# Attention softmax written to an SBUF page, and the splits of landed squares ordered behind it

## Chip, cores and metric

One core of a Trainium2 chip runs the whole program. The metric is the device time of one execution in microseconds (us). The engines are named as in the profile: PE multiplies matrices, DVE, ACT and POOL work on tiles elementwise, SP issues most DMAs. Each engine runs its instructions strictly in the order in which they stand in its own queue, and waits for the others through semaphores. PE writes to PSUM; DVE and ACT reach both PSUM and SBUF, POOL and the DMAs only SBUF in this kernel.

## Reference

A backbone of two layers over 1024 latent tokens of width 1024 and 256 context tokens, in float32. Layer 0 is windowed attention with a sink logit and 16 query heads on 4 key heads; layer 1 is a gated convolution module. The change touches the attention of layer 0 alone. Cut to what matters:

```python
def block_fn(args):                     # 128 queries of one block, all heads
    qblk, blk = args
    kw = ... # keys of blocks blk-1, blk, blk+1 (384 keys), vw likewise
    s_win = einsum(qblk, kw) * scale; s_win = where(mask, s_win, -inf)
    s_ctx = einsum(qblk, kc) * scale                     # 256 context keys
    p_ctx, p_win = sink_softmax(sink, s_ctx, s_win)      # one softmax over sink, context and window
    return einsum(p_ctx, vc) + einsum(p_win, vw)
...
y = (o * silu(z)) @ w_out
```

## The kernel before

Every float32 product is made of three matmuls on parts: a high part (the value rounded to PE's fp32r type, made by ACT with a copy) and a low part (the rest, made by DVE or POOL with a subtraction), as high*high + high*low + low*high.

**Blocks.** The attention stage walks `steps`, 16 heads x 8 query blocks (`h`, `qb`). A block goes through this chain. `scores` (L1096): six matmuls write 128 queries x up to 640 keys to a PSUM tile `pss` (two such tiles exist, used in turn). DVE scales and masks the scores and takes the maximum (a fused tensor_tensor_reduce, which the profile calls CUSTOM_DVE_ANT, result `sc`), ACT takes the exponential with its sum, DVE the reciprocal, ACT multiplies by it. All of this is done in place in `pss`. `square_up` (L1130): DVE transposes 32 x 32 squares from `pss` to an SBUF page `psq_page`, and a DMA writes that to DRAM (`psq`). `land` (L1149): a DMA reads it back with the squares in place, to one of four slots (qb mod 4) of the SBUF tile `ptlo`. `split_p` (L1155): ACT makes the high part `pthi`, and POOL (slots 0, 1) or DVE (slots 2, 3) the low part in place in `ptlo`; for blocks 3 and 4 a strip of 32 columns goes to `edge` pages as well. `pv` (L1188): when four blocks (a half of a head) are split, 18 matmuls multiply values by the probabilities, into `pso`. Four slots are all there is: the next half lands only when `pv` has read this one.

**Order.** In step i the loop of L1318 emits: `square_up(i)`, the landing of block i-2, `scores(i+1)`, the split of block i-3, then `fill(12)`, that is 12 matmuls of the projection of a later head (tile `psg`, with weight chunks `whi`, `wlo`; 24 matmuls make half a chunk, whose result ACT and DVE or POOL take away: `rope_half` for a query chunk, `zs_page` for a gate chunk), and after every fourth block `pv`. Beside this run the low parts of output weights (`lhi_page`, `low_page`) and sums for the second modulation (`pso<-dww_raw`). PE is pinned to the order of the program (`pin("P")`). On DVE, ACT, POOL and SP a list scheduler places the instructions, by its own estimate of when each can run. `after(ins, anchor)` (L661) ties an instruction behind another in that order, without a semaphore.

**Pages.** SBUF pages of 1024 floats come from a pool of 45, and the page that has been free longest is given out first.

At three places, where the key head changes (`regroup`, L1358, behind heads 3, 7 and 11), whole chunks of keys and values stand between the last scores of one group and its `pv`.

Of the kernel before, what the change touches and what calls it, by code (L numbers as in the profile page):

```python
# [9 lines left out]
F32 = mybir.dt.float32  # L10
F32R = mybir.dt.float32r
AF = mybir.ActivationFunctionType
ALU = mybir.AluOpType

P = 128
# [15 lines left out]
TB = T // P  # L31
# [64 lines left out]
def backbone_kernel(  # L96
# [8 lines left out]
    V, A, G, PE, SY = (InOrder(tc, e) for e in (nc.vector, nc.scalar, nc.gpsimd, nc.tensor, nc.sync))  # L105
# [10 lines left out]
    pg = Pages(pgpool, 45, "page", 1024)  # L116
# [8 lines left out]
    def ps_s():  # L125
        return ps.tile([P, 1024], F32, tag="s", name=nm("pss"), bufs=2)
# [18 lines left out]
    def ctile(shape, dt, name):  # L145
        return cpool.tile(shape, dt, tag=name, name=name, bufs=1)

    def small(shape, dt=F32, name="sm", bufs=2):
        return cpool.tile(shape, dt, tag=f"{name}", name=nm(name), bufs=bufs)

    def act(out, in_, func, **kw):
        return A.activation(out=out, in_=in_, func=func, **kw)

    def tt(eng, out, a, b, op):
        return eng.tensor_tensor(out=out, in0=a, in1=b, op=op)
# [4 lines left out]
    def split_lo(eng, lo, full, hi):  # L160
        return tt(eng, lo, full, hi.bitcast(F32), ALU.subtract)
# [5 lines left out]
    nsink = ctile([P, NH], F32, "nsink")  # L167
# [475 lines left out]
    mask = mask_pg[:, 0:768]  # L643
# [12 lines left out]
    anchor = []  # L656
    anchor_p = []
    anchor_a = []
    anchor_z = []

    def after(ins, anchor=anchor):  # L661
        if anchor:
            tc.add_manual_dep(ins.ins, anchor[0].ins.name, mybir.DependencyInfo(
                mybir.DependencyClass.NoSync, mybir.DependencyReason.DATA), reason="behind the softmax")
# [427 lines left out]
        fillq.append((key, job(key)))  # L1092

    ptile = {}

    def scores(h, qb):  # L1096
        g = h // 4
        q = qt[h]
        kk = kvt[g]
        c = kk[2]  # L1100
        k0, k1 = max(qb - 1, 0), min(qb + 1, TB - 1)
        nw = (k1 - k0 + 1) * P
        s = ps_s()
        w0 = 512 - nw
        qsl = slice(qb * P, qb * P + P)
        ksl = slice(k0 * P, k0 * P + nw)
        for n, (a, b) in enumerate(((0, 0), (0, 1), (1, 0))):
            PE.matmul(s[:, w0:512], q[a][:, qsl], kk[b][:, ksl], start=n == 0, stop=n == 2)
            PE.matmul(s[:, 512:768], q[a][:, qsl], c[:, b], start=n == 0, stop=n == 2)
        sc8 = small([P, 3], name="sc", bufs=6)  # L1110
        nmx, l0, ri = (sc8[:, i:i + 1] for i in range(3))
        w = nw + CT

        act(s[:, 768:769], nsink[:, h:h + 1], AF.Copy)
        sc = dict(scale=-SCALE, scalar=nsink[:, h:h + 1], op0=ALU.add, op1=ALU.min, accum_out=nmx)
        if qb == TB - 1:
            sv = s[:, w0:768].rearrange("p (a b) -> p a b", a=2)
            V.tensor_tensor_reduce(out=sv, in0=sv, in1=mask.rearrange("p (a b) -> p a b", a=2)[:, :, 0:256], **sc)
        else:
            V.tensor_tensor_reduce(out=s[:, w0:768], in0=s[:, w0:768], in1=mask[:, 640 - w:640], **sc)  # L1120
        act(s[:, w0:769], s[:, w0:769], AF.Exp, bias=nmx, scale=-1.0, accum_out=l0)
        V.reciprocal(ri, l0)
        act(s[:, w0:768], s[:, w0:768], AF.Copy, scale=ri)
        ptile[(h, qb)] = s
        if qb == TB - 1:
            pg.free(*qt.pop(h))

# [1 line left out]

    def square_up(h, qb):  # L1130

        s = ptile.pop((h, qb))
        sq = pg.alloc(F32, [1024], "psq")
        st = sq[:, 0:640].rearrange("p (b t j) -> p t b j", b=4, t=5)
        turns = {0: ((256, 1, 4),), TB - 1: ((256, 0, 2), (384, 2, 3))}.get(qb, ((128, 0, 5),))
        for c0, t0, nt in turns:
            anchor[:] = [V.transpose(out=st[:, t0:t0 + nt],
                                     in_=s[:, c0:c0 + nt * P].rearrange("p (t b j) -> p t b j", t=nt, b=4))]
        z = squares[(h * TB + qb) % len(squares)]
        x0 = 32 * int(qb == 0)  # L1140
        SY.dma_start(out=z.rearrange("(p b) x -> p b x", b=4)[:, :, x0:160],
                     in_=sq[:, 0:640].rearrange("p (b x) -> p b x", b=4)[:, :, x0:160])
        pg.free(sq)

    def slot(t, qb):
        x0, ql = 32 * int(qb == 0), qb % 4
        return t[:, ql * 640:ql * 640 + 640].rearrange("p (a x) -> p a x", a=4)[:, :, x0:160]
# [7 lines left out]
    def split_p(h, qb):  # L1155

        hi, lo = (slot(t, qb) for t in (pthi, ptlo))
        raw = lo.bitcast(F32)
        if qb in (3, 4):
            if h % 2 == 0 and qb == 3:  # L1160
                edges[:] = [pg.alloc(F32R, [2, 4, P], "edge")]
            i, t = 2 * (qb - 3) + 1 - h % 2, 64 * (4 - qb)
            eh, el = (edges[0][:, n, i].rearrange("p (a j) -> p a j", a=4) for n in range(2))
            act(eh, raw[:, :, t:t + 32], AF.Copy)
            split_lo(V, el, raw[:, :, t:t + 32], eh)
        anchor_a[:] = [act(hi, raw, AF.Copy)]
        if qb % 4 < LO_POOL:
            anchor_p[:] = [split_lo(G, lo, raw, hi)]
        else:
            anchor[:] = [split_lo(V, lo, raw, hi)]  # L1170

    edges = []

# [89 lines left out]
    for kt in range(KT):  # L1263
# [12 lines left out]
        if 0 < kt < 5:  # L1276
            for _ in range(2):
                b = (KT - len(ctodo)) % 3
# [15 lines left out]
        if kt == KT - 1:  # L1294
            scores(0, 0)
# [22 lines left out]
    for i, (h, qb) in enumerate(steps):  # L1318
# [14 lines left out]
        if nxt and nxt[1] == 0:  # L1333
            fill(1000, ("q", h + 1))
        square_up(h, qb)
        h2, q2 = back(i, 2)
        h3, q3 = back(i, 3)
# [3 lines left out]
        if nxt and not regroup:  # L1341
            scores(*nxt)
        if h3 >= 0 and h3 // 4 == h // 4:
            split_p(h3, q3)
# [13 lines left out]
        if regroup:  # L1358
            g = nxt[0] // 4
            old = kvt[g - 1]  # L1360
            land(h, qb - 1)
            run(job(("k", g)))
            land(h, qb)
            for q in range(qb - 2, qb + 1):
                split_p(h, q)
            run(job(("v", g)))
            pv(h, 1)
            pg.free(*old[:3])
            scores(*nxt)
            continue  # L1370
# [7 lines left out]
    h, qb = NH - 1, TB - 1  # L1378
    land(h, qb - 1)
    split_p(h, qb - 2)  # L1380
    land(h, qb)
    fill(12)
# [649 lines left out]
```

## Time and profile before

| | |
|---|---|
| median of 3 runs | 1804.7 us (1802.41 to 1808.81) |
| the profiled execution: its own time | 1810.56 us |
| its span on the core | 1807.9 us |
| DVE, ACT, POOL busy in the span | 67%, 54%, 49% |
| start of the first `pv` of the profile, start of the last | 110.21 us, 927.63 us |

The attention stage takes about 130 to 940 us of the span; the stages behind it are the output projection of the attention and the convolution layer. The profile is read as follows. A group row has the engine, the operation, the tile written and those read, the shape, the count, and after the bar the busy time in us, the mean time of one in ns, and how long the engine had stood idle before them, with what ended that idle time. A row of the timeline has the start and the length in us, and in square brackets the idle time before it. In a row of stretches each engine's busy time is followed by its number of instructions, and then the mean TensorE clock that was granted (PEclk, 1.00 is the full clock).

### The profile page before, as it was taken

Reading aid. Unit: us, or ns where it says so; the run is one execution under the profiler, and the core shown is the slowest. Engines: PE = TensorE matmul, PEld = TensorE weight load, DVE = VectorE, ACT = ScalarE, POOL = GpSimd, SP = SyncE. Lnnn points to the kernel's source line nnn. Section 1 sums busy time; section 2 is a strip of 40 time slices with the busy share of each in tenths; the row PEclk is TensorE's granted clock in tenths of the full one; section 3 lists DMA queues with packets and bytes.
Section 4 is the critical chain, followed back from the end, with each engine's and each line's share of the span. In section 5 each row is a group of like instructions: output and inputs, shape, how many; then the busy total and the mean of one; then the engine's idle time right before and its main releaser. Section 6 shows DMA issues by size and latency. Waiting matters only on the chain.

```text
span 1807.9 us, 23416 instructions
## 1 busy us (share of the span) xinstructions
PE 1666.5 (92%) x7828; PEld 1386.2 (77%) x7828; DVE 1216.5 (67%) x2227; ACT 972.1 (54%) x1699; POOL 890.6 (49%) x658
## 2 busy tenths in 40 slices
PE   9988799888988789888779999999999999999998
PEld 6776677777777678766668887888888888888887
DVE  5866765565466564567531528999999999986742
ACT  6755555555456554565523435565665656466651
POOL 0345654555545455363200116799988898420310
PEclk9999999988999989999889999999999999999999
DMA  9476766776468665767877762202020212277981
GB/s 380 138 226 221 245 193 195 230 229 217 146 200 265 213 194 171 236 211 213 279 228 268 250 239 82 94 13 82 13 82 24 82 47 67 85 238 230 344 293 59
DMA packets 206936, 326.31 MB, mean 180 GB/s; under 512 B 15722, under 2 KB 114338, under 8 KB 206816
## 3 DMA queue, kind: packets, MB, share of 16 engines
q1 hardware_dynamic: 200736, 314.86, 52.5%
q10 hardware_dynamic: 6080, 9.97, 2.1%
q8 instruction: 61, 1.00, 0.2%
q14 instruction: 59, 0.48, 0.1%
HBM read 231.70 MB, written 82.58 MB: 174 GB/s over the span
## 4 chain that ended last, share of the span: by engine, by line
PE 64%; DMA 17%; DVE 9%; ACT 6%; issue 3%; POOL 1%; SPq 0%; ACTq 0%; DVEq 0%; POOLq 0%
PE psg L90 31%; PE pso L90 18%; PE pss L90 16%; DMA ptlo<-psq 7%; DMA psq<-psq_page 4%; ACT pss L90 2%; DVE psq_page L90 2%; DVE pss L90 1%; ACT pthi L90 1%; DMA dww_raw<-in_ada_w_dram 1%; DMA low_page<-in_conv_w_out_dram 1%; DVE ptlo L90 1%; DVE pso L90 1%; DMA rope_half<-rope_half 1%; ACT lhi_page L90 1%
## 5 line engine op out<-in xcount | busy, mean ns | idle before, releaser
L90 POOL TENSOR_TENSOR odd_half<-odd_half,prod_half 128x513 f32<-128x513 f32 (+2 forms) x252 | 313.8, 1253 | 23.2 <-ACT prod_half L90 10.0
L90 POOL TENSOR_TENSOR wlo_page<-wraw_page,whi_page 128x512 fp32r<-128x512 f32 (+1 forms) x104 | 175.5, 1703 | 234.9 <-ACT whi_page L90 175.6
L90 PE MATMUL psg<-hh_page,whi_page 128*128 128x512 f32 x600 | 246.7, 411 | 0.6 <-DVE kvc_page L90 0.6
L90 PE MATMUL psg<-hl_page,whi_page 128*128 128x512 f32 x600 | 243.9, 407 | 0.0
L90 PE MATMUL psg<-hh_page,wlo_page 128*128 128x512 f32 x600 | 242.8, 405 | 0.0
L90 ACT ACTIVATE pss<-pss,sc 128x640 f32<-128x640 f32 (+3 forms) x256 | 187.5, 735 | 102.6 <-DVE sc L90 98.6
L90 ACT ACTIVATE prod_half<-ubuf,dww 128x513 f32<-128x513 f32 (+2 forms) x252 | 165.4, 675 | 115.5 <-POOL odd_half L90 111.6
L90 PE MATMUL psg<-h2h_page,whi_page 128*128 128x512 f32 x464 | 181.9, 392 | 0.0
L90 PE MATMUL psg<-h2h_page,wlo_page 128*128 128x512 f32 x464 | 180.6, 389 | 0.0
L90 PE MATMUL psg<-h2l_page,whi_page 128*128 128x512 f32 x464 | 180.5, 389 | 0.0
L90 DVE SCALAR_TENSOR_TENSOR pss<-ubuf,dww,pss 128x512 f32<-128x512 f32 (+3 forms) x270 | 172.5, 671 | 0.1
L90 DVE SCALAR_TENSOR_TENSOR pss<-ubuf,wsum,pss 128x512 f32<-128x512 f32 (+3 forms) x270 | 171.8, 671 | 0.2
L90 POOL TENSOR_TENSOR ptlo<-ptlo,pthi 128x512 fp32r<-128x512 f32 (+1 forms) x64 | 103.8, 1628 | 109.1 <-ACT pthi L90 62.2
L90 DVE STREAM_TRANSPOSE psq_page<-pss 128x640 f32<-128x640 f32 (+1 forms) x144 | 106.8, 752 | 68.6 <-ACT pss L90 56.0
L90 PE MATMUL pss<-kh_page,qh_page 128*128 128x384 f32 (+1 forms) x128 | 48.6, 380 | 102.8 <-DVE psq_page L90 79.7
L90 PEld LDWEIGHTS psg<-hh_page,wlo_page 128*128 128x128 f32 x600 | 118.5, 198 | 26.5
L90 PEld LDWEIGHTS psg<-hh_page,whi_page 128*128 128x128 f32 x600 | 120.3, 200 | 22.1 <-DVE kvc_page L90 1.0
L90 PEld LDWEIGHTS psg<-hl_page,whi_page 128*128 128x128 f32 x600 | 119.5, 199 | 20.5
L90 ACT ACTIVATE whi_page<-wraw_page 128x1024 fp32r<-128x1024 f32 x88 | 92.7, 1053 | 69.4 <-PE psg L90 26.4
L90 ACT ACTIVATE pthi<-ptlo 128x640 fp32r<-128x640 f32 (+1 forms) x128 | 91.1, 718 | 58.8 <-DMA ptlo<-psq 57.2
L90 POOL TENSOR_TENSOR low_page<-low_page,lhi_page 128x512 f32<-128x512 f32 x64 | 89.8, 1409 | 63.0 <-ACT lhi_page L90 46.4
L90 PEld LDWEIGHTS pss<-kh_page,qh_page 128*128 128x128 f32 x128 | 25.5, 199 | 123.9 <-issue 115.2
(267 smaller groups left out, 4193.7 us busy)
## 6 DMA issues: line engine op xcount, KB each, us to landing
psq<-psq_page SPq DMA_DIRECT2D x112, 320.0 KB, 4.0
ptlo<-psq SPq DMA_DIRECT2D x112, 320.0 KB, 5.1
wraw_page<-in_k_wconv_dram SPq DMA_DIRECT2D x48, 512.0 KB, 3.7
wraw_page<-in_k_win_dram SPq DMA_DIRECT2D x40, 512.0 KB, 4.3
wol_page<-wolA SPq DMA_DIRECT2D x32, 512.0 KB, 8.3
wo_page<-in_attn_w_out_dram SPq DMA_DIRECT2D x32, 512.0 KB, 6.6
wo_page<-in_conv_w_out_dram SPq DMA_DIRECT2D x32, 512.0 KB, 6.6
wol_page<-wolC SPq DMA_DIRECT2D x32, 512.0 KB, 6.8
```

The source lines that it names most:

```text
L90: r = f(*a, **k)
```

## The change

The masked scores are now written by the fused reduce to an SBUF page `p` (allocated in `scores`, freed in `square_up`); the exponential and the scaling by the reciprocal, both still on ACT, run in place in that page, and the transposes read it. PSUM holds the raw scores only until the reduce has read them. The sink's column is put at the end of the page. Two lists name the newest softmax's reciprocal (`tie_v`, DVE) and scaling (`tie_a`, ACT): the splits on ACT and DVE, and the next block's sink column, are tied behind them. The splits on POOL are not tied. What is computed is the same.

```diff
+    tie_v, tie_a = [], []
...
-        act(s[:, 768:769], nsink[:, h:h + 1], AF.Copy)
+        p = pg.alloc(F32, [1024], "p")
+        after(act(p[:, w:w + 1], nsink[:, h:h + 1], AF.Copy), tie_a)
...
-            V.tensor_tensor_reduce(out=s[:, w0:768], in0=s[:, w0:768], in1=mask[:, 640 - w:640], **sc)
-        act(s[:, w0:769], s[:, w0:769], AF.Exp, bias=nmx, scale=-1.0, accum_out=l0)
-        V.reciprocal(ri, l0)
-        act(s[:, w0:768], s[:, w0:768], AF.Copy, scale=ri)
-        ptile[(h, qb)] = s
+            V.tensor_tensor_reduce(out=p[:, 0:w], in0=s[:, w0:768], in1=mask[:, 640 - w:640], **sc)
+        act(p[:, 0:w + 1], p[:, 0:w + 1], AF.Exp, bias=nmx, scale=-1.0, accum_out=l0)
+        tie_v[:] = [V.reciprocal(ri, l0)]
+        tie_a[:] = [act(p[:, 0:w], p[:, 0:w], AF.Copy, scale=ri)]
+        ptile[(h, qb)] = p
...
-                                     in_=s[:, c0:c0 + nt * P].rearrange("p (t b j) -> p t b j", t=nt, b=4))]
+                                     in_=p[:, c0:c0 + nt * P].rearrange("p (t b j) -> p t b j", t=nt, b=4))]
+        pg.free(p)
...
-            act(eh, raw[:, :, t:t + 32], AF.Copy)
-            split_lo(V, el, raw[:, :, t:t + 32], eh)
+            after(act(eh, raw[:, :, t:t + 32], AF.Copy), tie_a)
+            after(split_lo(V, el, raw[:, :, t:t + 32], eh), tie_v)
         anchor_a[:] = [act(hi, raw, AF.Copy)]
+        after(anchor_a[0], tie_a)
...
             anchor[:] = [split_lo(V, lo, raw, hi)]
+            after(anchor[0], tie_v)
```

The order on PE is the same before and after. On ACT, DVE, POOL and SP most rows of the attention stage move. The first place is ACT where head 9 begins, in the order of before: `pss_6641` is its block 0, `pss_6680` its block 1, and the four rows with `pthi` (one of them twice) split blocks 4 to 7 of head 8.

```order
L90 ACTIVATE pss_6641,sc_6648<-pss_6641,sc_6648 128x513
L90 ACTIVATE edge_page_6578<-ptlo 128x128
L90 ACTIVATE pthi<-ptlo 128x640
L90 ACTIVATE lhi_page_1337<-low_page_6620 128x512
L90 ACTIVATE pss_6641<-pss_6641,sc_6648 128x512
L90 ACTIVATE pthi<-ptlo 128x640
L90 ACTIVATE lhi_page_1337<-low_page_6620 128x512
L90 ACTIVATE pss_6680<-nsink 128x1
L90 ACTIVATE qh_page_6435<-rope_half_6627 128x512
L90 ACTIVATE pthi<-ptlo 128x640 x2
L90 ACTIVATE zs_page_6658<-psg_6659 128x512
L90 ACTIVATE pss_6680,sc_6687<-pss_6680,sc_6687 128x641
```

The same place of the changed kernel, where `p_page_6753` is block 0 and `p_page_6793` block 1 of head 9:

```order
L90 ACTIVATE qh_page_6536<-rope_half_6731 128x512
L90 ACTIVATE p_page_6753,sc_6752<-p_page_6753,sc_6752 128x513
L90 ACTIVATE p_page_6753<-p_page_6753,sc_6752 128x512
L90 ACTIVATE edge_page_6682<-ptlo 128x128
L90 ACTIVATE pthi<-ptlo 128x640
L90 ACTIVATE lhi_page_1347<-low_page_6724 128x512
L90 ACTIVATE p_page_6793<-nsink 128x1
L90 ACTIVATE p_page_6793,sc_6792<-p_page_6793,sc_6792 128x641
L90 ACTIVATE p_page_6793<-p_page_6793,sc_6792 128x640
L90 ACTIVATE pthi<-ptlo 128x640
```

Four splits stood ahead of the exponential of block 1; now one stands there, and the four are spread out, one behind the softmax of each block. The second place is ACT at block 3 of head 9, the last block before the `pv` of head 8's second half, before:

```order
L90 ACTIVATE pss_6762,sc_6769<-pss_6762,sc_6769 128x641
L90 ACTIVATE zs_page_6658<-psg_6739 128x512
L90 ACTIVATE pss_6762<-pss_6762,sc_6769 128x640
L90 ACTIVATE whi_page_6917<-wraw_page_6532 128x1024
L90 ACTIVATE ozs_page_6614<-zs_page_6658 128x256
```

and now, with `p_page_6877` as that block and `psg_6846` as the half chunk whose last matmul stands right ahead of that `pv` on PE:

```order
L90 ACTIVATE p_page_6877,sc_6876<-p_page_6877,sc_6876 128x641
L90 ACTIVATE whi_page_7028<-wraw_page_6635 128x1024
L90 ACTIVATE zs_page_6763<-psg_6846 128x512
L90 ACTIVATE p_page_6877<-p_page_6877,sc_6876 128x640
L90 ACTIVATE pthi<-ptlo 128x640
L90 ACTIVATE lhi_page_1347<-low_page_6859 128x512
```

The split of head 8's block 7 stood ahead of the exponential of block 1; now it is behind the scaling of this block, and a weight chunk's high part has come between the exponential and the scaling. The third place is DVE in the same block of the changed kernel (ISA is the fused reduce and the reading of its result):

```order
L90 ISA p_page_6877,sc_6876<-pss_6869,mask_page_597,nsink 128x640
L90 ISA sc_6876 128x1
L90 STREAM_TRANSPOSE psq_page_6866<-p_page_6829 128x5x4x32
L90 TENSOR_TENSOR ptlo<-ptlo,pthi 128x640
L90 SCALAR_TENSOR_TENSOR pso_951<-dww_raw,cs,pso_951 128x256
L90 RECIPROCAL sc_6876<-sc_6876 128x1
L90 SCALAR_TENSOR_TENSOR pso_951<-wsum_raw,cs,pso_951 128x256
L90 COPY mask_page_597<-pso_951 128x256
L90 SCALAR_TENSOR_TENSOR zs_page_6763<-zs_page_6763,psg_6846 128x512
L90 STREAM_TRANSPOSE psq_page_6925<-p_page_6877 128x5x4x32
L90 TENSOR_TENSOR ptlo<-ptlo,pthi 128x640
```

The low part of block 7 (the last row) now stands behind the reciprocal and the transpose of this block; before, both DVE low parts of that half stood ahead of the reciprocal of block 1.

More of the change, by code (lines that the diff above doesn't have):

```diff
@@ L1112, in scores @@
         w = nw + CT
-        act(s[:, 768:769], nsink[:, h:h + 1], AF.Copy)
+        p = pg.alloc(F32, [1024], "p")
+        after(act(p[:, w:w + 1], nsink[:, h:h + 1], AF.Copy), tie_a)
         sc = dict(scale=-SCALE, scalar=nsink[:, h:h + 1], op0=ALU.add, op1=ALU.min, accum_out=nmx)
         if qb == TB - 1:
-            sv = s[:, w0:768].rearrange("p (a b) -> p a b", a=2)
-            V.tensor_tensor_reduce(out=sv, in0=sv, in1=mask.rearrange("p (a b) -> p a b", a=2)[:, :, 0:256], **sc)
-        else:
-            V.tensor_tensor_reduce(out=s[:, w0:768], in0=s[:, w0:768], in1=mask[:, 640 - w:640], **sc)
-        act(s[:, w0:769], s[:, w0:769], AF.Exp, bias=nmx, scale=-1.0, accum_out=l0)
-        V.reciprocal(ri, l0)
-        act(s[:, w0:768], s[:, w0:768], AF.Copy, scale=ri)
-        ptile[(h, qb)] = s
+            V.tensor_tensor_reduce(
+                out=p[:, 0:w].rearrange("p (a b) -> p a b", a=2),
+                in0=s[:, w0:768].rearrange("p (a b) -> p a b", a=2),
+                in1=mask.rearrange("p (a b) -> p a b", a=2)[:, :, 0:256],
+                **sc)
+        else:
+            V.tensor_tensor_reduce(out=p[:, 0:w], in0=s[:, w0:768], in1=mask[:, 640 - w:640], **sc)
[3 more added lines that the diff above has]
+        ptile[(h, qb)] = p
         if qb == TB - 1:
@@ L1130, in square_up @@
     def square_up(h, qb):
-        s = ptile.pop((h, qb))
+        p = ptile.pop((h, qb))
         sq = pg.alloc(F32, [1024], "psq")
         st = sq[:, 0:640].rearrange("p (b t j) -> p t b j", b=4, t=5)
-        turns = {0: ((256, 1, 4),), TB - 1: ((256, 0, 2), (384, 2, 3))}.get(qb, ((128, 0, 5),))
+        turns = {0: ((0, 1, 4),), TB - 1: ((0, 0, 2), (128, 2, 3))}.get(qb, ((0, 0, 5),))
         for c0, t0, nt in turns:
             anchor[:] = [V.transpose(out=st[:, t0:t0 + nt],
-                                     in_=s[:, c0:c0 + nt * P].rearrange("p (t b j) -> p t b j", t=nt, b=4))]
+                                     in_=p[:, c0:c0 + nt * P].rearrange("p (t b j) -> p t b j", t=nt, b=4))]
+        pg.free(p)
         z = squares[(h * TB + qb) % len(squares)]
```

## The prediction

> **What bounds the kernel now.** I read the page first, then the stretch of the attention stage, then who PE waited for in it, and last the timeline at single waits.
>
> ```profile
> span 1807.9 us, 23416 instructions
> ...
> PE 1666.5 (92%) x7828; PEld 1386.2 (77%) x7828; DVE 1216.5 (67%) x2227; ACT 972.1 (54%) x1699; POOL 890.6 (49%) x658
> ```
>
> ```profile
> 130.00:940.00 810.00, 686.43 (x3286) 579.28 (x3286) 473.30 (x932) 426.73 (x860) 392.33 (x289) 0.93 0.68 215
> ```
>
> PE carries the program. All but a little of its idle time lies in the attention stage: 810.00 - 686.43 = 123.6 us of 1807.9 - 1666.5 = 141.4 us. No other engine is full there (DVE 473 of 810), so the loss is one of latency. The waits of PE in that stage, with total, number and longest:
>
> ```profile
> PE pss L90 <- DVE psq_page L90: 74.7, 31, 5.2
> PE pss L90 <- DVE sc L90: 19.3, 6, 5.3
> ...
> PE pso L90 <- DVE ptlo L90: 7.8, 2, 4.2
> ```
>
> 94.0 us are scores that wait for a `pss` tile, to be released by the transposes of the block two before. 7.8 us are `pv` waiting for a low part. Why the transposes are late shows at the start of head 9 on ACT and DVE:
>
> ```profile
> 544.00 0.31 ACT L90 ACTIVATE edge_page<-ptlo 128x128 fp32r<-128x128 f32 x1 [2.11 <-DMA ptlo<-psq]
> 544.21 0.72 ACT L90 ACTIVATE pthi<-ptlo 128x640 fp32r<-128x640 f32 x1
> 544.84 0.61 ACT L90 ACTIVATE lhi_page<-low_page 128x512 fp32r<-128x512 f32 x1
> 545.36 0.64 ACT L90 ACTIVATE pss<-pss,sc 128x513 f32<-128x513 f32 x1
> ```
>
> ```profile
> 555.87 0.41 PE L90 MATMUL pss<-kh_page,qh_page 128*128 128x384 f32 x1 [3.31 <-DVE psq_page L90]
> ```
>
> ACT stood 2.11 us at a split whose square had not landed, and the exponential behind it in the queue waited too. The delay runs through block 1 to its transpose, and PE stands 3.31 us at the scores of block 3.
>
> A wait costs more than its length. Stretches right behind a wait, then the wait that stood ahead of the second of them:
>
> ```profile
> 152.30:157.70 5.40, 5.40 (x16) 4.53 (x17) 1.81 (x5) 3.13 (x6) 1.80 (x2) 0.50 0.64 218
> 172.20:175.60 3.40, 3.40 (x17) 2.99 (x18) 3.27 (x8) 1.45 (x5) 1.03 (x1) 1.00 0.70 237
> 219.50:222.50 3.00, 3.00 (x10) 2.71 (x11) 3.00 (x6) 1.78 (x5) 2.00 (x2) 0.50 0.58 171
> 384.90:389.80 4.90, 4.90 (x14) 4.22 (x15) 2.17 (x6) 1.83 (x4) 0.41 (x1) 0.50 0.82 255
> 557.10:560.50 3.40, 3.40 (x10) 2.66 (x9) 1.28 (x3) 1.58 (x4) 1.57 (x2) 0.50 0.43 152
> ```
>
> ```profile
> 172.16 0.41 PE L90 MATMUL pss<-kh_page,qh_page 128*128 128x384 f32 x1 [2.73 <-DVE psq_page L90]
> 152.27 0.55 PE L90 MATMUL pss<-kh_page,qh_page 128*128 128x256 f32 x1 [3.96 <-DVE psq_page L90]
> ```
>
> Behind waits of 3.31 and 3.96 us the granted clock is 0.50 for 3.0 to 5.4 us, mean of the four rows with 0.50: 4.2 us, in which half of the time is lost, 2.1 us. Behind 2.73 us it stays 1.00. The stage's mean clock of 0.93 says the same in total: (1 - 0.93) / 0.5 x 810 = 113 us at half clock, so about 57 us lost. The block waits are 101.8 of the 123.6 us idle, so 82% of that, 47 us, is theirs. **At stake: 101.8 + 47 = 149 us.**
>
> A second way: three halves of heads, from one `pv` to another.
>
> ```profile
> 132.55 0.40 PE L90 MATMUL pso<-pthi,kvc_page 128*128 128x512 f32 x1
> ...
> 203.97 0.40 PE L90 MATMUL pso<-pthi,kvc_page 128*128 128x512 f32 x1
> 207.14 0.28 PE L90 MATMUL pss<-kh_page,qh_page 128*128 128x256 f32 x1
> ```
>
> ```profile
> 564.35 0.33 PE L90 MATMUL pss<-kh_page,qh_page 128*128 128x384 f32 x1
> ...
> 565.23 0.40 PE L90 MATMUL psg<-hh_page,whi_page 128*128 128x512 f32 x1
> ...
> 567.96 0.33 PE L90 MATMUL pss<-kh_page,qh_page 128*128 128x384 f32 x1
> ```
>
> (203.97 - 132.55) / 3 = 23.8 us a half. Without waits, scores take 565.23 - 564.35 = 0.88 us and the 12 fill matmuls 2.73, so a step is 3.61 and a half 4 x 3.61 + 3.17 for `pv` + some 0.5 of other matmuls = 18.1 us. Lost: 5.7 us a half. Of 32 `pv`, three stand behind a regroup; 29 x 5.7 = 165 us. I take the middle of the two, **157 us, 5.4 us a half**.
>
> **The change, part by part.** *Removed: the wait of scores for transposes.* The `pss` tile is free when the reduce has read it, and that reduce belongs to a block two steps (7.2 us) older. I cost what is left at nothing; the cover is those two steps.
>
> *Added: the wait of `pv` for the split of its fourth block.* The last split is now tied behind the softmax of the block whose scores stand one fill ahead of `pv`. In that order, on ACT and DVE:
>
> ```profile
> L90 DVE CUSTOM_DVE_ANT_0 pss<-pss,mask_page,nsink 128x640 f32<-128x640 f32 x88 | 77.4, 880 | 23.5 <-ACT pss L90 22.6
> L90 ACT ACTIVATE pthi<-ptlo 128x640 fp32r<-128x640 f32 x105 | 75.9, 730 | 31.2 <-DMA ptlo<-psq 29.8 <-issue 1.2
> L90 DVE TENSOR_TENSOR ptlo<-ptlo,pthi 128x640 fp32r<-128x640 f32 x60 | 75.1, 1255 | 16.9 <-ACT pthi L90 16.2
> L90 DVE STREAM_TRANSPOSE psq_page<-pss 128x640 f32<-128x640 f32 x89 | 74.8, 844 | 39.4 <-ACT pss L90 33.0 <-DMA psq<-psq_page 6.0
> L90 ACT ACTIVATE pss<-pss,sc 128x641 f32<-128x641 f32 x88 | 67.1, 762 | 40.5 <-DVE sc L90 39.5
> L90 ACT ACTIVATE pss<-pss,sc 128x640 f32<-128x640 f32 x88 | 66.8, 762 | 40.1 <-DVE sc L90 38.5 <-DMA wraw_page<-in_k_win_dram 0.9 <-DVE pso L90 0.5
> ...
> L90 ACT ACTIVATE whi_page<-wraw_page 128x1024 fp32r<-128x1024 f32 x33 | 34.8, 1055 | 20.0 <-DVE oz_half L90 8.3 <-PE psg L90 7.1 <-DMA wolC<-low_page 2.1
> ...
> L90 ACT ACTIVATION_READ_ACCUMULATOR pss<-pss,sc 128x1 f32 x117 | 22.7, 194 | 0.0
> ...
> L90 DVE RECIPROCAL sc<-sc 128x1 f32<-128x1 f32 x117 | 18.3, 156 | 59.4 <-ACT pss L90 58.4
> ...
> L90 ACT ACTIVATE zs_page<-psg 128x512 f32<-128x512 f32 x29 | 17.1, 589 | 11.5 <-PE psg L90 11.5
> L90 DVE DVE_READ_ACCUMULATOR2_ANT sc<- 128x1 f32 x117 | 16.2, 139 | 0.0
> ```
>
> From the start of the scores: 1.0 until they are written, reduce 0.88 + 0.14, exponential 0.76 + 0.19, reciprocal 0.16, scaling 0.76, high part 0.73, low part 1.26, and eight handovers of about 0.05: 6.3 us. `pv` would be due after 3.61. So the gap is at least 2.7 us. Two instructions stand between exponential and scaling in the new order on ACT. The tanh of the gate half chunk (0.59) or the copy of the query half chunk waits for the last fill matmul at 3.6 and ends at 4.3, where the scaling could have begun at 3.3: +1.0, gap 3.7. The weight chunk's high part (1.06) runs from 3.1 to 4.2 and pushes that by 0.5: 4.2. On DVE the reciprocal stands behind a transpose (0.84) and a low part (1.26) of the block before; where that block is itself late, this adds up to 0.8: 5.0. A queued transpose of 0.84 runs beside the high part. I take **4.2 us**, with 3.2 and 5.0 as ends, the lower one where no weight chunk is in the way and the low part is a short one. Every such gap is above 3.1, so the half clock follows: 2.1 us, ends 1.7 and 2.7 (halves of 3.4 and 5.4). It falls on the 18 matmuls of `pv`, which then free the four slots later, so nothing hides it. 29 x (4.2 + 2.1) = 183 us; ends 29 x 4.9 = 142 and 29 x 7.7 = 223.
>
> *Behind `pv`.* On PE the next scores queue behind it; on SP the four landings wait for it, and on ACT the splits for those. That loop now contains all four softmaxes in a row. One block there takes exponential to reciprocal 1.1, scaling 0.76, transpose 0.84, next reduce 1.02, about 3.8 us with handovers against PE's 3.61, so the last block is at most a few tenths late; this is inside the upper end.
>
> *Moved to SBUF.* The exponential and scaling in SBUF are not in the trace; the nearest row is `pthi`, 730 ns for the same width from SBUF to SBUF, so 0.03 us less each, at most 29 x 0.06 = 2 us. The transpose from SBUF could lie between
>
> ```profile
> L90 DVE SCALAR_TENSOR_TENSOR zs_page<-zs_page,psg x29: 648/682/689, 132.0 to 876.2; 128x512 f32<-128x512 f32 x29
> L90 DVE TENSOR_TENSOR ptlo<-ptlo,pthi x60: 784/1218/2248, 144.6 to 922.8; 128x640 fp32r<-128x640 f32 x60
> ```
>
> (least, median, largest ns): steady with one input in SBUF, scattered up to 2248 with two. The transpose has one; I leave it at 0.84. If it scattered like the second row (mean 0.4 above the least), each of the 29 last blocks would be that much later, +12 us; if it went to the first row's 0.8 for 640 columns, nothing changes.
>
> [...]
>
> *Pages.* One page more is in use and 128 more are given out, so a page is reused sooner. A reduce may wait until a DMA has read the page's last tenant; landed DMAs take 3.8 us in the median against 3.6 of a step. I take 0 with an end of +10 us.
>
> **Sum.** -157 + 183 - 2 = +24 us; I take off 4 for halves where the gap is nearer its lower end: +20. The profiled execution took 1810.56, 5.9 above the median of 1804.7, so 1830.6 in its frame and **1825** in that of the median.
>
> **Rivals.** *A, faster.* The last softmax runs with nothing in its way, the gap stays at its floor of 2.7 to 3.2 and the clock drops behind half of them: 29 x (3.0 + 1.05) = 117, -40 us, **1765**. For it: a wait of 2.73 us kept the full clock, and the scheduler's order puts the tanh there only because it expects the fill to be done. Against: in that order ACT has no choice. It decides from 157 / 29 = 5.4 us a half, a gap of about 3.4. *B, equal.* The gap is 3.4 to 3.8 and what PE saves at the scores it loses at `pv`: **1805**. *C, the change does not do what it says.* The scores still wait, now for a reduce that stands on DVE behind other blocks' low parts; a third of the 94 us stays and `pv` waits too: 1825 + 31 + 10 for the clock, **1866**.
>
> **Chances.** Forecast 0.55, A 0.25, B 0.14, C 0.06. The forecast's own range is 1804.7 - 157 + 142 = 1790 to 1804.7 - 157 + 223 = 1871 with most of it above 1805. Over all cases I give 1768 to 1862: it takes in A nearly to its middle and leaves out C and the far upper end. A difference of 0.3% (5.4 us) is about what a measurement of this kernel can tell from no change. Faster 0.27 (A and 0.02 of the forecast's lower end), same 0.14 (B), slower 0.59 (the rest of the forecast, and C).
>
> **What would show it.** In the changed profile PE's waits before `pss` should be under 10 us in the stage. PE's wait before `pso` for `ptlo` should have some 29 entries of 3 to 5 us, sum 95 to 145. PEclk should be 0.50 in most `pv`. The rows of exponential and scaling should be near 730 ns. The forecast is wrong if the `pv` waits sum to less than 90 us, if they are mostly under 2.8 us long, or if scores still wait.

## The result, and the profile after

The changed kernel takes **1896.0 us** (1890.85 to 1900.98, 4 runs) against 1804.0 us (1802.41 to 1808.81, 4 runs): ratio 1.0505 [1.0468, 1.0542]. It is slower, as forecast, but by 92 us instead of 20, and outside the range. The profiled execution took 1900.98 us with a span of 1899.2 us.

The stretch of the attention stage, which now ends some 90 us later, and the stretch behind it (length, then busy time and count of PE, PEld, DVE, ACT, POOL, then the granted clock, the DMA share, GB/s):

```profile
130.00:1020.00 890.00, 698.89 (x3244) 585.97 (x3243) 467.99 (x933) 444.31 (x870) 392.16 (x284) 0.88 0.62 194
1020.00:1890.00 870.00, 868.11 (x3898) 718.73 (x3897) 655.68 (x1101) 458.11 (x677) 464.41 (x346) 1.00 0.41 140
```

Behind the stage nothing is lost: PE is busy in 868 of 870 us at full clock. In it PE idles 191 us (890.00 - 698.89) and the clock is 0.88. Who PE waited for there (total, times, longest):

```profile
PE pso L90 <- ACT pthi L90: 141.4, 27, 9.2
PE pso L90 <- DVE ptlo L90: 34.9, 27, 4.2
PE psg L90 <- ACT ozh_page L90: 8.8, 2, 8.4
```

The 94 us of waits before `pss` are gone entirely; there is no such row any more. In their place `pv` waits 176 us, first for a high part (ACT), then for a low part (DVE). And what `pv` does behind the wait is slow. The same group of PE in the kernel before (first row) and in the changed one (second):

```profile
L90 PE MATMUL pso<-pthi,kvc_page 128*128 128x512 f32 x128 | 46.4, 404 | 0.0
```

```profile
L90 PE MATMUL pso<-pthi,kvc_page 128*128 128x512 f32 x128 | 72.5, 615 | 148.8 <-ACT pthi L90 148.8
```

615 ns for one matmul instead of 404. The 32 `pv`, from first matmul to last without the waits inside, took 112 us in all before and 176 us now, 2.0 us more each.

One of the longest waits is that of `pv` of head 8's second half. It is not the half of the third piece of order above: all three pieces there are of head 13, not of head 9. (At head 9 the timeline in the prediction has the strip and the first split ahead of the exponential of 513 columns; the first piece has them behind it.) PE, ACT and DVE from the start of the scores of block 3 of head 9 (start, length, instruction, idle time before it):

```profile
607.13 0.33 PE L90 MATMUL pss<-kh_page,qh_page 128*128 128x384 f32 x1
...
607.95 0.84 DVE L90 STREAM_TRANSPOSE psq_page<-p_page 128x640 f32<-128x640 f32 x1 [0.96 <-ACT p_page L90]
...
608.72 1.53 DVE L90 TENSOR_TENSOR ptlo<-ptlo,pthi 128x640 fp32r<-128x640 f32 x1
...
609.59 0.35 SPq L90 DMA_DIRECT2D wolC<-low_page  x1
...
611.56 0.69 DVE L90 SCALAR_TENSOR_TENSOR zs_page<-zs_page,psg 128x512 f32<-128x512 f32 x1 [0.39 <-ACT zs_page L90]
...
615.98 0.20 ACT L90 ACTIVATE p_page<-nsink 128x1 f32<-128x1 f32 x1 [3.28 <-DMA wolC<-low_page]
616.11 0.88 DVE L90 CUSTOM_DVE_ANT_0 p_page<-pss,mask_page,nsink 128x640 f32<-128x640 f32 x1 [3.86 <-DMA wsum_raw<-in_ada_w_dram]
616.91 0.08 DVE L90 DVE_READ_ACCUMULATOR2_ANT sc<- 128x1 f32 x1
617.09 0.83 ACT L90 ACTIVATE p_page<-p_page,sc 128x641 f32<-128x641 f32 x1 [0.91 <-DVE sc L90]
...
618.25 0.83 ACT L90 ACTIVATE p_page<-p_page,sc 128x640 f32<-128x640 f32 x1 [0.23 <-DVE sc L90]
618.98 0.72 ACT L90 ACTIVATE pthi<-ptlo 128x640 fp32r<-128x640 f32 x1
...
619.75 0.80 PE L90 MATMUL pso<-pthi,kvc_page 128*128 128x512 f32 x1 [8.86 <-ACT pthi L90]
```

From the reduce on (616.11) the chain takes 3.6 us to `pv`, the sum of the forecast's terms for it. But the reduce starts 9.0 us behind the start of its scores, where the forecast had 1.0. Until 612.25 it stands in DVE's queue, behind the transpose and the low part of the block before and other work; then it waits 3.86 us more. Both writers of the new page, ACT's sink column and DVE's reduce, start at 616.0: the page's last tenant was a `low_page` of output weights, whose store to DRAM (`wolC`) was issued at 609.59 and had first to be read out. The name in DVE's bracket is only the last of several releases; ACT's row, which writes the same page at the same moment, names the right one.

Over the 28 `pv` that wait (the three behind a regroup and the last of all don't), read off the trace one by one: the reduce of the newest block starts **3.9 us** behind its scores on the mean, and the gaps, inside `pv` too, are **6.6 us** on the mean. At block 3 of head 13, the place of the pieces of order, the reduce stands ahead of the transpose of the block before and starts 1.1 us behind its scores, and the gap is 3.5 us. It stands so in 12 of the 28 halves; in the other 16 it is behind that transpose.

### The profile page after: what moved, and what is told of

The parts are those of the page before. It is cut to its first block, busy times and chain, and to the rows that moved or that the text cites. A ratio compares the mean times of both kernels' runs of the same rounds, so it can differ in the third digit from the quotient of the medians.

```text
span 1899.2 us, 23538 instructions
## 1 busy us (share of the span) xinstructions
PE 1687.0 (89%) x7828; PEld 1399.6 (74%) x7828; DVE 1208.4 (64%) x2227; ACT 985.8 (52%) x1699; POOL 886.2 (47%) x658
## 4 chain that ended last, share of the span: by engine, by line
PE 56%; DMA 5%; DVE 5%; ACT 3%; issue 2%; POOL 1%; ACTq 0%; SPq 0%; DVEq 0%; POOLq 0%
PE psg L90 27%; PE pso L90 17%; PE pss L90 13%; DMA psq<-psq_page 3%; ACT p_page L90 1%; DVE ptlo L90 1%; DVE psq_page L90 1%; DVE p_page L90 1%; DMA ptlo<-psq 1%; POOL rope_half L90 0%; DVE x_page L90 0%; DMA wolC<-low_page 0%; DVE pso L90 0%; DMA dww_raw<-in_ada_w_dram 0%; DMA wsum_raw<-in_ada_w_dram 0%
## 5 line engine op out<-in xcount | busy, mean ns | idle before, releaser
L90 ACT ACTIVATE p_page<-p_page,sc 128x640 f32<-128x640 f32 (+3 forms) x256 | 205.5, 803 | 196.6 <-DVE sc L90 193.4
L90 PE MATMUL psg<-hh_page,whi_page 128*128 128x512 f32 x600 | 235.9, 393 | 0.0
L90 PE MATMUL psg<-hl_page,whi_page 128*128 128x512 f32 x600 | 234.2, 390 | 0.0
L90 PE MATMUL psg<-hh_page,wlo_page 128*128 128x512 f32 x600 | 233.6, 389 | 0.0
L90 PE MATMUL pso<-pthi,kvc_page 128*128 128x512 f32 x128 | 72.5, 615 | 148.8 <-ACT pthi L90 148.8
L90 DVE STREAM_TRANSPOSE psq_page<-p_page 128x640 f32<-128x640 f32 (+1 forms) x144 | 106.8, 750 | 89.6 <-ACT p_page L90 57.9
L90 PEld LDWEIGHTS pso<-pthi,kvc_page 128*128 128x128 f32 x128 | 37.7, 294 | 166.5 <-ACT pthi L90 160.6
L90 PEld LDWEIGHTS psg<-hh_page,whi_page 128*128 128x128 f32 x600 | 112.9, 188 | 19.0 <-ACT hh_page L90 0.3
L90 ACT ACTIVATE woh_page<-wo_page 128x1024 fp32r<-128x1024 f32 x63 | 66.3, 1055 | 103.3 <-DMA wo_page<-in_conv_w_out_dram 35.6
L90 PE MATMUL pso<-h2h_page,whi_page 128*128 128x512 f32 x304 | 118.3, 389 | 0.0
```

Source lines behind the costliest of these rows:

```text
L90: r = f(*a, **k)
```

## The experiments

T1 says that the ties are the loss; T2 that the page is. In the table, "gap" is the mean wait of those 28 `pv`, "reduce" the mean time from the start of the newest scores to their reduce, and "behind" in how many of the 28 halves that reduce stands behind the transpose of the block before on DVE. Ratios are to the kernel before, run on the same chip. The times are of several chips, on which the kernel before took 1804 to 1810 us, so a difference between two times is good to some 5 us.

| kernel | us | ratio [95%] | gap | reduce | behind |
|---|---|---|---|---|---|
| the change | 1896.0 | 1.0505 [1.0468, 1.0542] | 6.6 | 3.9 | 16 |
| ties in PSUM | 1918.4 | 1.0620 [1.0563, 1.0678] | 6.5 | 4.9 | 28 |
| the same, column free | 1870.5 | 1.0339 [1.0299, 1.0379] | 5.1 | 2.4 | 9 |
| column on DVE | 1885.4 | 1.0424 [1.0384, 1.0464] | 6.1 | 3.8 | 17 |
| last split tied | 1877.8 | 1.0403 [1.0365, 1.0441] | 5.8 | 4.4 | 11 |
| odd tile, idle page | 1851.3 | 1.0260 [1.0215, 1.0305] | 5.0 | 1.4 | 2 |
| tile for even blocks | 1850.0 | 1.0249 [1.0220, 1.0278] | 4.9 | 2.3 | 6 |
| tile for odd blocks | 1825.0 | 1.0090 [1.0059, 1.0121] | 4.3 | 1.2 | 2 |
| ties on DVE only | 1820.1 | 1.0082 [1.0056, 1.0108] | 4.1 | 4.2 | 16 |
| first three tied | 1810.4 | 1.0014 [0.9990, 1.0038] | 3.7 | 6.3 | 14 |
| ties one block older | 1780.2 | 0.9848 [0.9804, 0.9893] | 2.8 | 4.4 | 11 |
| page, no ties | 1764.1 | 0.9754 [0.9708, 0.9801] | 1.6 | 6.7 | 12 |

The time follows the gap, but for the second row. A late reduce costs most where the last split is tied behind it: without ties it is later than in any other row, and the kernel the fastest. In the kernel before, the gap is 0.3 us, but the reduce already starts 2.4 us behind its scores, and stands behind that transpose in 17 of the 28 halves.

**The page without ties.**

```diff
-        after(act(p[:, w:w + 1], nsink[:, h:h + 1], AF.Copy), tie_a)
+        act(p[:, w:w + 1], nsink[:, h:h + 1], AF.Copy)
...
-        after(anchor_a[0], tie_a)
...
-            after(anchor[0], tie_v)
```

(and the same for the two edge strips)

> The SBUF page stays, all five ties are taken out. Theory T1 (the ties hold the last split of a half behind the softmax of the block in work, and pv waits for it: 28 gaps of 6.3 us, then the half clock): the gaps before pv behind pthi and ptlo lose most of their 176 us, the mean clock of the attention stage comes back from 0.88 to 0.92 or more, and with the scores no longer waiting for transposes the time is 1740 to 1805. Theory T2 (the page itself: 830 ns instead of 762 for exponential and scaling, and waits until a page's last tenant has been read): the time stays above 1840. Theory T3 (the loop through the four slots closes the same loss at pv, ties or not): 1795 to 1820, with the waits before pss of the kernel before now standing before pso, some 100 us.

Measured 1764.1 us, 2.5% under the kernel before. T1 holds, T2 and T3 fall. PE's waits for `pthi` and `ptlo` in the stage, and its stretch:

```profile
PE pso L90 <- DVE ptlo L90: 23.9, 13, 5.9
PE pso L90 <- ACT pthi L90: 15.7, 5, 7.8
```

```profile
130.00:1020.00 890.00, 798.64 (x3871) 673.91 (x3871) 507.18 (x1011) 486.31 (x929) 404.97 (x299) 0.95 0.74 236
```

40 us are left of the 176, the clock is 0.95, and PE works 799 us in the same stretch instead of 699. The page alone is worth 40 us; all five ties together cost 132 us on top of it.

**The ties without the page.** `after` with `tie_a` and `tie_v` as in the change, in the kernel before.

> The kernel before (softmax in place in PSUM) with the same five ties. T1: as slow as the changed kernel or nearly so, 1870 to 1900, with some 28 waits before pso of 5 to 6.5 us; the shorter passes on ACT (762 for 830 ns, two a block) take at most 0.15 us off each gap and the clock's share of it, some 5 us. T2: the ties alone cost what the prediction gave them, gaps near 4.2 us, 1805 to 1840.

1918.4 us, above the band of T1: the ties are the loss, more even than in the changed kernel. The gap is 6.5 us here without any page, so pages could not be the only way to a late softmax. Why, is told below.

**Ties one block older.**

```diff
-        tie_v[:] = [V.reciprocal(ri, l0)]
-        tie_a[:] = [act(p[:, 0:w], p[:, 0:w], AF.Copy, scale=ri)]
+        tie_v[:], tie_a[:] = tie_n[0:1], tie_n[1:2]
+        tie_n[:] = [V.reciprocal(ri, l0), act(p[:, 0:w], p[:, 0:w], AF.Copy, scale=ri)]
```

> The changed kernel, but a split is tied behind the softmax one block older than the newest. T1: the split that pv waits for may start one step, 3.6 us, earlier: the gaps before pv fall from a mean of 6.3 us to under 3, the clock behind most of them stays full, and the time is 1730 to 1800. T2: the pages and the longer passes are as before, the time stays above 1840.

1780.2 us: one step of 3.6 us more room takes 3.8 us off the gap. The tie to the newest block is what hurts, not a tie as such.

**PE kept busy ahead of `pv`.**

```diff
+        for _ in range(12):
+            PE.matmul(o, kh[:, 0:P], kh[:, 0:512], start=True, stop=True)
         pv_mm(o, work)
```

> The changed kernel with 12 matmuls of 512 columns on a key page, written to the bank that pv then overwrites, ahead of each pv (some 4.7 us of PE work that nobody reads). If the half clock behind the gaps comes from PE standing idle for 3 us and more: the idle time before pv falls from 6.3 to some 2 us a gap, the stage's mean clock rises from 0.88 to 0.95 or more, pv takes 3.2 us again instead of 5.6, and the time falls by 30 to 60 us to 1835 to 1865 although the same chain is waited for; where a gap is shorter than 4.7 us it costs up to 1 us. If the half clock has another cause, the time stays at 1890 or more.

```profile
130.00:1020.00 890.00, 772.57 (x3669) 649.40 (x3668) 471.71 (x940) 444.59 (x868) 390.38 (x291) 0.92 0.63 197
```

1885.6 us (1.0433 [1.0384, 1.0483]), 10 us less instead of 30 to 60. The 12 matmuls followed each other at 0.23 us and took 2.9 us, not the 4.7 expected, and `pv` still waited 105 us; the clock rose only to 0.92, and the 32 `pv` took 153 us instead of 176. The 13 `pv` with at most 2.14 us of wait left ran at a granted clock of 1.00, the 19 with 2.25 us or more at 0.50 to 0.83. So here the half clock goes with the idle PE, but this run removes only a third of its cost, and it pays 2.9 us at the four `pv` that did not wait.

**Which tie.** The ties on ACT alone give no other kernel: without the two DVE ties every engine's order comes out as in the changed kernel. The other way round:

```diff
-        after(anchor_a[0], tie_a)
```

(and without the ties of the strip's high part and the column)

> The changed kernel with the ties on DVE alone (low parts behind the newest reciprocal); the high parts and the sink column on ACT are free. If the tie on ACT carries the loss, with the scaling and the high part in the chain (some 1.6 us) and the exponential's queue behind it: gaps before pv under 3 us on the mean, the clock mostly full, 1770 to 1830. If the low part's tie alone is enough, since it too waits for the exponential of the newest block: 1860 or more.

1820.1 us: the time lies in the first band, but the gap is 4.1 us and not under 3. The ties on DVE alone cost 56 us over the kernel without ties. By slot, `after(anchor_a[0], tie_a if qb % 4 == 3 else [])` and the like:

> The changed kernel, but only the split of slot 3 (and block 3's edge strip) and the sink column are tied; slots 0 to 2 are free. The same chain stands ahead of pv. Theory L (the newest softmax is 2.9 us late because the splits of the other three slots are tied too, so that softmaxes and splits of a half run in one single file): the gap falls to the 4.2 us of the prediction, and the time is 1800 to 1850. Theory D (the lateness comes from the pages and from copies that stand ahead of the exponential, whatever the other ties): 1870 to 1900.

1877.8 us, by theory D: freeing the other three slots takes 18 us, the reduce stays 4.4 us late. And `qb % 4 < 3`:

> The changed kernel with slots 0 to 2 tied and slot 3 free. pv then waits at most for the softmax one block older, as in the run with ties one block older. If the tie of the last split carries the loss: 1750 to 1800, gaps before pv under 3 us on the mean. If the ties of the other three slots are enough to close the loop: 1830 or more.

1810.4 us, between the two bands, with a gap of 3.7 us. The sink column is tied in both runs. With it the tie of the last split costs 114 us over the 1764 of the kernel without ties, the ties of the other three 46; all together cost 132, so the two overlap.

**The pages.** SBUF has room for one small tile more, so every second block can be taken out of the pool.

```diff
-        p = pg.alloc(F32, [1024], "p")
+        p = cpool.tile([P, 648], F32, tag="p", name=nm("p"), bufs=1) if qb % 2 else pg.alloc(F32, [1024], "p")
```

> The changed kernel with all ties, but the softmax of every odd block is written to a tile of its own instead of a page of the pool, so half of the 128 extra pages are not given out and that tile's last tenant is long transposed. The newest block ahead of every pv is odd (3 or 7). If the 2.9 us by which the reduce of that block starts later than the prediction had it come from pages still being read by a DMA or another engine: the gaps before pv fall from 6.3 to 4 to 5 us and the time by 30 to 60 us, to 1835 to 1865. If pages play a small part: 1880 to 1900.

1825.0 us, with every tie in place: 71 us of the 92 are gone, more than the band had. The same half as above, h9 block 3, here:

```profile
615.73 0.33 PE L90 MATMUL pss<-kh_page,qh_page 128*128 128x384 f32 x1
...
616.81 0.88 DVE L90 CUSTOM_DVE_ANT_0 p<-pss,mask_page,nsink 128x640 f32<-128x640 f32 x1 [0.17 <-PE pss L90]
...
618.78 0.83 ACT L90 ACTIVATE p<-p,sc 128x641 f32<-128x641 f32 x1
...
622.61 0.72 ACT L90 ACTIVATE pthi<-ptlo 128x640 fp32r<-128x640 f32 x1
...
623.39 0.79 PE L90 MATMUL pso<-pthi,kvc_page 128*128 128x512 f32 x1 [3.88 <-ACT pthi L90]
```

The reduce stands ahead of the transpose of the block before and waits only for PE, 1.1 us behind the start of its scores; the wait ahead of `pv` is 3.88 us, not 8.86. PE's waits in the stage:

```profile
PE pso L90 <- ACT pthi L90: 76.8, 26, 5.4
PE pso L90 <- DVE ptlo L90: 38.2, 27, 3.4
```

Two runs ask whether it is the newest block's own page or the rhythm of the pool. First the tile for the even blocks (`qb % 2 == 0`), second the tile for the odd ones with a page taken and given back beside it, unused:

> The changed kernel with all ties, and the tile of its own goes to the even blocks; the newest block ahead of every pv (3 or 7) uses a page of the pool again. Theory N (what costs is that the newest block's own page is not free, so its reduce is queued behind the transpose and the low part of the block before): the gaps stay near 6 us and the time at 1870 to 1900. Theory P (what costs is the pool as a whole, 128 pages more given out, whichever block gets them): as with the odd blocks, 1815 to 1850, gaps of 4 to 4.7 us.

> All ties; the odd blocks' softmax in the tile of its own as in the run at 1825 us, but each odd block also takes a page of the pool at the same place and gives it back at the same place, and nothing is written to it. So the pool hands out its pages in the rhythm of the changed kernel, and only the newest block itself is free of them. Theory N (what costs is the wait of that block's reduce for its own page): 1815 to 1840 as with the tile alone, its reduce some 1.2 us behind the start of its scores. Theory P (what costs is that all pages come round sooner: squares, weights, low parts): 1870 to 1900, the reduce late again.

1850.0 and 1851.3 us: neither theory alone. Relieving the pool without the newest block saves 46 us, relieving the newest block in the old rhythm 45, both together 71.

**The same two tiles without ties.**

> No ties, and the odd blocks' softmax in the tile of its own. If the pages cost as much without ties as with them (71 us): about 1695. If a late softmax is mostly hidden when no split is tied to it: 1735 to 1764, since only the waits of scores and pv for late blocks (70 us in the run without ties) can shrink, by a third at best. If the tile's own reuse two blocks later is a new wait: above 1770.

> No ties, and the even blocks' softmax in the tile of its own. Without ties no block is special ahead of pv, so this should equal the run without ties with the odd tile within 10 us, 1735 to 1764. If the two differ by more, the order that the scheduler happens to find is worth that much, and differences of this size between the other runs say nothing of the mechanism.

1776.7 us (0.9839 [0.9813, 0.9864]) and 1757.1 (0.9746 [0.9713, 0.9779]), on either side of 1764.1. Without ties the pages cost nothing that these runs can show. The two runs differ by some 20 us, and why is not shown: it may be the scheduler's order by itself, or the tile's own reuse two blocks later, which the first expectation names. From 130 to 900 us ACT waits 25.5 us in 27 places until the transposes have read the odd tile, 11.2 us in 15 for the even one. Either way the split of the 71 us above is no finer than 20 us.

**The sink column.** In PSUM the reduce never starts before ACT has written the sink column to the same tile (0 of 127 blocks); on the page it does in 64 of 127. It is the program that asks for it: in PSUM each reduce waits for a semaphore of ACT (22.6 of the 23.5 us of idle time ahead of the reduces in the prediction's first row end with it), on the page none does (126 of the 128 wait for PE). With the column tied behind the scaling of the block before, the PSUM run has its softmaxes in single file. One half of it on ACT and DVE:

```profile
623.70 0.77 ACT L90 ACTIVATE pss<-pss,sc 128x640 f32<-128x640 f32 x1 [0.23 <-DVE sc L90]
...
624.50 0.85 DVE L90 STREAM_TRANSPOSE psq_page<-pss 128x640 f32<-128x640 f32 x1 [0.83 <-ACT pss L90]
625.02 0.16 ACT L90 ACTIVATE pss<-nsink 128x1 f32<-128x1 f32 x1
625.27 0.78 DVE L90 TENSOR_TENSOR ptlo<-ptlo,pthi 128x640 fp32r<-128x640 f32 x1
...
626.36 0.89 DVE L90 CUSTOM_DVE_ANT_0 pss<-pss,mask_page,nsink 128x640 f32<-128x640 f32 x1
```

Scaling of one block, column of the next, and its reduce behind the transpose and the low part. Untying only the column there, and in the changed kernel writing it on DVE (`V.tensor_copy`), untied:

> The kernel before with the ties of the splits, but the sink column is not tied. If the column's tie puts the softmaxes of the PSUM run in single file (the reduce waits for the column, which waits for the scaling of the block before): the reduce of the newest block no longer stands behind the low part in 28 of 28 halves, the gaps fall from 6.5 to 4 to 5 us, and the time from 1918 to 1830 to 1870. If the column plays no part: 1900 to 1925.

> The changed kernel with the splits tied, the softmax on pages, and the sink column written by DVE instead of ACT, untied. If the page costs because ACT's queue stands at the column until the page is free (the waits of ACT before p_page for psq, wolA, wolC and wlo, some 17 us, ahead of exponentials and splits): 1840 to 1870, gaps of 4.5 to 5.5 us. If it costs through the reduce on DVE, which waits for the same page: 1880 to 1900.

In PSUM 48 us go, to 1870.5, at the upper edge of the expected band: the column's tie was that much of the PSUM run. In the changed kernel only 11 us go, to 1885.4: on the page it is mostly the reduce on DVE that costs, not ACT standing at the column. Last, the column on DVE without ties, with the tile for the even blocks and with pages for all:

> No ties, even blocks in the tile of their own, sink column by DVE. ACT loses 128 columns of 0.19 us and its 17 us of waits for pages at them, DVE gains 128 short copies of some 0.1 us. If late softmaxes still set what PE waits for in the stage: 1735 to 1753, faster than 1757 by what ACT saves ahead of the exponentials. If ACT's queue is not the limit without ties: 1750 to 1770.

> No ties, all blocks on pages, sink column by DVE. As the run before, beside the 1764 us of the run without ties: 1740 to 1758 if the column on ACT costs, 1758 to 1775 if not. The difference between this and the run before shows how much the order by itself moves the time.

1755.2 (0.9708 [0.9663, 0.9753]) and 1754.4 us (0.9705 [0.9661, 0.9748]): the fastest of all, though the intervals overlap with those of 1764.1 and 1757.1, so what the column adds is not shown.

## Why the prediction was wrong in size

**Right: what goes.** Scores wait for no transpose any more, 0 us against a test of under 10. What it freed agrees too, taken by subtraction: `pv` waits and slow `pv` added 178 us of gaps (185 against 8 over the program) and 64 us of half clock, 242 in all, and the stage's last `pv` ends 91 us later (1022.1 against 931.0); so 151 us were freed elsewhere. The forecast freed 157, of which 8 were waits of `pv`: 149.

**Right: what comes, and why.** `pv` waits for the split behind the newest softmax, in 28 halves where 29 were counted. The sign to look for named the low part alone, with a sum of 95 to 145 us; the trace has 141.4 us for the fourth block's high part ahead of `pv` and 34.9 us for its low part inside `pv`, together 176. The half clock was sized well: 64 us over the 28 that wait, 2.3 us each, against 2.1. The 3.1 us above which the forecast let it follow are no sharp line in the trace: in the attention stage of the kernel before, each wait of PE of 3.15 us or more was followed by a stretch at 0.50, but so was one of 2.76 us (ahead of 331.94 us), while 2.73 kept 1.00.

**Wrong: the gap, 6.6 us for 4.2, and the step behind it is "Pages".** Its sentence was "I take 0 with an end of +10 us". 28 x 2.4 = 67 us, nearly all of the 71 that were missing. The terms from the reduce on held on the mean (6.4 us from the reduce to the end of the waits, 6.8 in the forecast); the first one, "1.0 until they are written", measured 3.9, because the reduce was not free to start when the scores were there. It waits until a DMA has read the page's last tenant (in 7 of 28 halves a DMA ends the idle time right before it), or stands in DVE's queue behind the transpose and the low part of the block before (16 and 13 of 28 halves; 2 and 0 with the tile for the odd blocks). The chain of the forecast was read at head 13, where the reduce stands ahead of that transpose.

The mean hides two kinds of halves. In the 16 with the reduce behind that transpose it starts 5.6 us behind its scores and the gap is 7.2 us; in the other 12 it starts 1.8 us behind them and the gap is still 5.9 us. In some of these the wait for a page comes later in the chain: ahead of the `pv` at 458.9 us the transpose in front of the reciprocal waits 3.61 us for its `psq_page`, by its row until a DMA has read an earlier one.

A page is not the only way to a late reduce. In the kernel before it starts 2.4 us behind its scores, a number that stood in the trace; with the ties in PSUM and the column free it is 2.4 us too, without any page, with a gap of 5.1 us and 1870.5 us. Of the runs with all ties only the two with the odd tile, at 1.2 and 1.4 us, come near the 1.0 of the forecast. I had compared a landing's median with a step and asked only whether the reduce waits, not that `pv` waits for this very reduce in every half, so that its delay is paid 28 times, in full. With half of the extra pages gone the measured time is 1825.0 us and the gap 4.3, which are the forecast's 1825 and 4.2: the agreement is closer than the 20 us by which two such runs differ without a known cause, so part of it is luck; it shows which term failed, not that every other was exact to a few us.

**"Behind `pv`" cannot be told apart from it.** That loop was costed at tenths. With the odd tile the reduce was 0.2 us later than forecast, so no more came from it there; in the run with only the last split tied the reduce stayed late with the loop cut open.

**Moved to SBUF: sign wrong, size small.** Exponential and scaling on the page, and the transposes (least, median, largest ns):

```profile
L90 ACT ACTIVATE p_page<-p_page,sc x256: 705/830/839, 79.4 to 991.1; 128x641 f32<-128x641 f32 x96, 128x513 f32<-128x513 f32 x32
L90 DVE STREAM_TRANSPOSE psq_page<-p_page x144: 436/841/848, 81.3 to 992.2; 128x640 f32<-128x640 f32 x96, 128x512 f32<-128x512 f32 x16, 128x256 f32<-128x256 f32 x16, 128x384 f32<-128x384 f32 x16
```

830 ns against 762 in PSUM, 0.07 us more each, where I had taken 730 from `pthi`, whose copy has another output type and neither bias nor scale operand: the wrong row. It is 29 x 0.14 = 4 us instead of -2. The transposes stayed at 0.84, as taken: 843 ns for 640 columns from the page, 844 from PSUM.

**The rivals.** A and B needed a gap under 3.8 us; the gap was 3.8 or less in 5 of 28 halves. C needed waits of scores; there were none. What was missing is a fourth rival: that the newest softmax itself starts late.

**Still open.** How the 71 us divide between the newest block's own page and the pool's rhythm; why the reduce stays 4.4 us late with three slots untied; what makes the 20 us between the odd and the even tile without ties; and how much the half clock costs by itself, since the busy matmuls filled only part of the gap.

## What to carry to other kernels

A tie in the order is a wait: follow it to the engine that waits at the end and ask how much room the step has there; here one step of room turned a loss of 5% into a gain of 1.5%, and no tie at all into one of 2.5%. A new buffer from a shared pool brings its last tenant's readers into the chain, and on a chain that some engine waits for in every round that is costed at the tenant's DMA, not at zero. Read a new order at more than one place: the half that was read had its reduce in time, 16 of 28 had not. Take apart a change that does two things: this one held a gain of 40 us and a loss of 132.

## What the runs showed of the hardware that was not expected

- ACT took longer from SBUF to SBUF than within PSUM for the same shapes: exponential and scaling of 640 columns 830 ns against 762. The sink column, read from SBUF, took 187 ns to SBUF against 169 to PSUM.
- Matmuls of 512 columns, 0.39 us long in the trace of the kernel before, follow each other there at 0.23 us at a granted clock of 1.00 (12 of the fill in 2.73 us); the 12 matmuls ahead of `pv` took 2.9 us.
- The clock stayed at half through most of a `pv` behind a wait: one matmul of 512 columns took 615 ns on the mean of 128, against 404. In the changed kernel 27 of the 28 `pv` that waited ran at a mean granted clock of 0.50 to 0.70, the other, behind 2.8 us of wait, at 1.00.
